# Order of the loads and sums at the head of an encoder kernel: x first, modulation pair by pair, half of the bias marks on ScalarE

## The chip, the cores and the metric

The kernel runs on one core of one Trainium2 chip. The metric is the time of one execution on the device in microseconds (us). Before the change it was 2237.97 us, the median of three runs (2234.70, 2237.97, 2239.76). The execution whose profile is shown here took 2236.12 us, and its span from the first to the last instruction was 2234.3 us.

## The reference, cut to what matters

The reference is a two-layer encoder trunk on 256 tokens of width 2048 in float32. Each sub-layer is modulated by a vector c. Only the parts that the change touches are given:

```python
cond = silu(c)
for l in range(2):
    mod = cond @ w_ada[l] + b_ada[l]              # 2048 -> 6 * 2048
    sh_a, sc_a, g_a, sh_m, sc_m, g_m = split(mod, 6)
    h = rmsnorm(x) * (1 + sc_a) + sh_a
    proj = h @ w_in[l]                            # 2048 -> 3904
    ...
    rel = positions[None, :] - positions[:, None]
    bias = rel_bias_table[t5_bucket(rel)]         # 32 buckets, 4 heads, same in both layers
    p = softmax(q @ k.T * scale + bias)
```

The bucket of a distance is found from its sign and its size. Distances 0 to 7 have a bucket each; the larger ones share buckets by ranges up to 128.

## The kernel before, in words

The 2048 features stand as 16 slices of 128 on the partitions, the 256 tokens on the free axis. The kernel is a stream of weights from HBM: SyncE (SP) issues nearly every DMA, in program order, into a ring of five tiles of 1 MB named `raw` (line 113 and 289). ScalarE (ACT) makes the upper part `hi` of each weight tile, VectorE (DVE) the rest `lo`, and TensorE (PE) multiplies the operand with both (lines 146, 147 and 182 to 184). A scheduler orders the instructions of each engine by its own forecast and puts in the semaphores; each engine then runs its list in order.

**Modulation.** `w_ada` is 192 tiles of 128 x 2048, and each is read once. DVE multiplies a tile with `cond` and sums along the row (`ada`, line 297), which gives 128 entries of one modulation vector; two such sums and a small addition (`mod`, lines 311 and 313) serve two slices. `ada_need` loads the tiles that the next step lacks, `ada(n)` loads n tiles in any case.

**Head.** `setup` loads c (`c_row`), spreads silu(c) over all partitions with four matmuls and four activations (`cond`, line 343), loads the small tables, then four `ada` tiles (`self.ada(4)`), then x in four parts, takes the squares of x on ACT (line 477) and their sums on DVE (line 478), and then ten more `ada` tiles (`LEAD`). The 14 tiles serve the shift and scale of slices 0 to 6.

**First input projection.** `norm_then_by_k` makes 1/rms (`rstd`, PE, ACT and DVE) and goes over eight pairs of slices, p = 0 to 7. Each pair needs four `ada` sums (two of the shift, two of the scale), then `modulated`: `ht` on DVE, `h` on ACT and DVE, and for p < 6 (`WHOLE`) `hf` on ACT. For these six pairs the weights are not split: four tiles `w` of 128 x 768 (line 228) go into PE as float32 (line 239), into buffers of the `hi` and `lo` tags. From p = 6 on they go through `hi` and `lo`.

**Fills.** After each pair one piece of setup is written: `lb` (lambdas, the start of the bias), then the four parts 0 to 3 of the bias, then the rope tables `r`. A part (`bias_part`) clamps the distances `rel` on DVE, and for eight groups of four buckets takes a square around the middle of the bucket (`sq`, ACT, line 428), compares it with the half width on DVE (a mark `oh` of 0 or 1, line 430) and multiplies the marks with the table on PE (lines 432 and 433). Four activations (line 435) then copy the result from PSUM to `bias`.

**Afterwards.** With p = 5 and 6, pieces of a later projection (`w_d`) are inserted; then come the remaining projections of layer 0 (`w_t`), interleaved with the attention scores (`psc`, line 943), which read k copied by ACT (line 272). From about 260 us on the kernel is a stream of weights whose order the change leaves as it is.

Of the kernel before, what the change touches and what calls it, by code (L numbers as in the profile page):

```python
# [13 lines left out]
AF = mybir.ActivationFunctionType  # L14
ALU = mybir.AluOpType
# [5 lines left out]
D = 2048  # L21
# [22 lines left out]
C_CB = 160  # L44
C_W2 = 168
# [26 lines left out]
def consts():  # L72
    c = np.zeros((P, NCONST), np.float32)
    p = np.arange(P)
    c[p, C_DELTA + p % 32] = 1.0
    c[p, C_PERM + (p ^ 32)] = 1.0
    for g in range(8):
        for r in range(4):
            b = 4 * g + r
            n = b % 16  # L80
            lo, hi = BUCKET_FROM[n], BUCKET_FROM[n + 1] - 1
            sign = -1.0 if b < 16 else 1.0
            rows = slice(32 * r, 32 * r + 32)
            if b == 16:
                c[rows, C_CB + g], c[rows, C_W2 + g] = 0.0, -1.0
            else:
                c[rows, C_CB + g] = -sign * (lo + hi) / 2.0
                c[rows, C_W2 + g] = ((hi - lo) / 2.0 + 0.25) ** 2
    c[:, C_FREQ] = np.asarray(INV_FREQ, np.float32)[p % 32]
    c[:, C_SGN] = np.where(p % 64 < 32, -1.0, 1.0)  # L90
    return c


EARLY = {5: (0,), 6: (1, 2)}
LEAD = 10
WHOLE = 6
NAHEAD = 6
NNORM = 12
# [6 lines left out]
class Trunk:  # L105
    def __init__(self, ctx, tc, io):
        self.nc, self.tc, self.io = tc.nc, tc, io
        pool = lambda name, bufs, **k: ctx.enter_context(tc.tile_pool(name=name, bufs=bufs, **k))
        self.fp = pool("fp", 1)
        self.wp = pool("wp", 4)  # L110
        self.up = pool("up", 40)
        self.tp = pool("tp", 6)
        self.cp = pool("cp", 1)
        self.sp = pool("sp", 8)
        self.ap = pool("ap", 6)
        self.pp = pool("pp", 8, space=bass.MemoryType.PSUM)
        self.ada_todo, self.ada_here, self.rate, self.credit = [], [], 0.0, 0.0
        self.n = 0

    def name(self, s):  # L120
        self.n += 1
        return f"{s}_{self.n}"
# [169 lines left out]
    def ada_sums(self, after=None):  # L292

        nc = self.nc
        for w, l, g, i in self.ada_here:
            acc = self.macc[l, g]
            ins = nc.vector.scalar_tensor_tensor(  # L297
                w, w, 1.0, self.cond, ALU.mult, ALU.mult, accum_out=acc[:, i : i + 1]
            )
            if after is not None:  # L300
                self.tc.add_manual_dep(
                    ins.ins, after.ins.name,
                    mybir.DependencyInfo(mybir.DependencyClass.NoSync, mybir.DependencyReason.DATA),
                    reason="issue order",
                )
            if i % 2:
                c = slice(i - 1, i + 1)
                v = V_BADA + 96 * l + NK * g + i
                b = self.vec[:, v - 1 : v + 1]
                if g % 3 == 1:  # L310
                    nc.vector.scalar_tensor_tensor(self.mod[l, g][:, c], acc[:, c], 1.0, b, ALU.add, ALU.add)
                else:
                    nc.vector.tensor_tensor(self.mod[l, g][:, c], acc[:, c], b, ALU.add)
        self.ada_here = []
# [14 lines left out]
    def setup(self):  # L329
        nc, io, cp = self.nc, self.io, self.cp  # L330
        self.ada_plan()
        self.cond = cp.tile([P, D], F32, name="cond")
        row = self.wp.tile([1, D], F32, tag="raw", name="c_row", bufs=5)
        nc.sync.dma_start(row, io["c"])
        self.mean = {}
        for n in (D, 2 * P):
            self.mean[n] = cp.tile([P, P], F32, name=f"mean{n}")
            nc.gpsimd.memset(self.mean[n], 1.0 / n)
        for j in range(4):
            c = slice(512 * j, 512 * j + 512)  # L340
            ps = self.bank("pc").rearrange("p a b -> p (a b)")
            nc.tensor.matmul(ps, self.mean[D][:1], row[:, c], start=True, stop=True)
            nc.scalar.activation(self.cond[:, c], ps, AF.Silu, scale=float(D))  # L343
        self.vec = cp.tile([P, NVEC], F32, name="vec")
        nc.sync.dma_start(self.vec, io["vec"])
        self.eps = cp.tile([P, 1], F32, name="eps")
        nc.gpsimd.memset(self.eps, EPS)
        self.K = cp.tile([P, NCONST], F32, name="K")
        nc.sync.dma_start(self.K, io["consts"])
        self.pos = cp.tile([P, T + 8], I32, name="pos")  # L350
        nc.sync.dma_start(self.pos, io["pos"])
        self.ident = cp.tile([P, P], F32, name="ident")
        make_identity(nc, self.ident)
        self.x = cp.tile([P, NK, T], F32, name="x")
        self.ada(4)
        for q in range(4):
            nc.sync.dma_start(self.x[:, 4 * q : 4 * q + 4], io["xT"][:, 4 * q : 4 * q + 4])
        acc = None
        for k in range(0, NK, 2):
            acc = self.sumsq(acc, self.x[:, k : k + 2])  # L360
        self.ada(LEAD)
        return acc

    def fills(self):
        m = {"l": self.lambdas, "r": self.rope_setup, "b": self.bias_setup}
# [45 lines left out]
    def bias_part(self, a):  # L411
        nc, K = self.nc, self.K
        fh, fl, lh, ll = self.bt
        half = lambda s, dt=F32: self.up.tile([P, 2 * T], dt, tag="u", name=self.name(s))
        r = self.u("rel")
        for t in range(2):
            j = 2 * a + t
            d = self.tp.tile([P, T], F32, tag="t", name=self.name("rt"))
            nc.vector.tensor_scalar(d, fh[:, :T], fh[:, T + j : T + j + 1], 65536.0, ALU.subtract, ALU.mult)
            nc.vector.scalar_tensor_tensor(  # L420
                r[:, t], fl[:, :T], fl[:, T + j : T + j + 1], d, ALU.subtract, ALU.add
            )
        nc.vector.tensor_scalar(r, r, -128.0, 128.0, ALU.max, ALU.min)
        ps = self.bank("pb")
        out = ps.rearrange("p a b -> p (a b)")
        for g in range(8):
            sq = self.t("sq")
            nc.scalar.activation(sq, r, AF.Square, bias=K[:, C_CB + g : C_CB + g + 1])
            oh = half("oh", F32R)
            nc.vector.tensor_scalar(oh, sq.rearrange("p a b -> p (a b)"), K[:, C_W2 + g : C_W2 + g + 1], None, ALU.is_le)  # L430
            c = slice((g % 4) * P, (g % 4) * P + P)
            nc.tensor.matmul(out, lh[g // 4][:, c], oh, start=g == 0, stop=False)
            nc.tensor.matmul(out, ll[g // 4][:, c], oh, start=False, stop=g == 7)
        for h in range(HD):
            nc.scalar.activation(self.bias[32 * a : 32 * a + 32, h], ps[32 * h : 32 * h + 32], AF.Copy, scale=-1.0)

    def rope_setup(self):
        nc, K, pos = self.nc, self.K, self.pos
# [115 lines left out]
    def modulated(self, r, k, sh, sc, whole=None):  # L554

        nc = self.nc
        t = self.t("ht")
        out = [self.parts("h") for _ in range(2)]
        for i, (hi, lo, _) in enumerate(out):
            c = slice(k + i, k + i + 1)  # L560
            nc.vector.scalar_tensor_tensor(t[:, i], self.x[:, k + i], sc[:, c], r, ALU.mult, ALU.mult)
            nc.scalar.activation(hi, t[:, i], AF.Identity, bias=sh[:, c])  # L562
            nc.vector.scalar_tensor_tensor(lo, t[:, i], sh[:, c], hi.bitcast(F32), ALU.add, ALU.subtract)  # L563
        if whole is not None:
            f = self.u("hf")
            for i in range(2):
                nc.scalar.activation(f[:, i], t[:, i], AF.Identity, bias=sh[:, k + i : k + i + 1])
                whole.append(f[:, i])
        return out

    def latent(self, vals, g):
# [15 lines left out]
    def norm_then_by_k(self, l, acc, sh, sc, src, n, nwhole, fill=(), early=()):  # L587


        r = self.rstd(acc, D)  # L590
        banks = self.open_banks(2 * n)
        h = []
        for p in range(8):
            k = 2 * p
            for g in (sh, sc):
                self.ada_need(l, g, k + 1)
            whole = [] if p < nwhole else None
            h += self.modulated(r, k, self.mod[l, sh], self.mod[l, sc], whole)
            self.by_k(banks, [src[l, p, b] for b in range(2)], h, k, NK, 2 * n, whole)
            if fill:  # L600
                fill.pop(0)()
            if p in early:
                early[p](h)
        return h, banks
# [532 lines left out]
```

## Time and profile before

| | |
|---|---|
| median of three runs | 2237.97 us (2234.70 to 2239.76) |
| profiled execution, its span | 2236.12 us, 2234.3 us |
| PE busy, share of the span | 2157.3 us, 97% |
| DVE busy | 1618.6 us, 72% |
| ACT busy | 1151.2 us, 52% |
| DMA | 585.40 MB, mean 262 GB/s |
| mean granted TensorE clock | 0.994 |

The times are those of one execution, taken by the hardware profiler. A row of the timeline gives the start and the length in us, the engine, the line of the kernel, the operation, the output and the inputs, the number of merged instructions, and in brackets how long the engine sat idle before it and what ended that. A row with several instructions gives the time from the first start to the last end. Consecutive instructions of one engine overlap a little, so the step from start to start is shorter than a length. A row by stretches gives the stretch, its length, the busy time of PE, PE's weight loads, DVE, ACT and GpSimd (with instructions), the granted clock, the busy share of the DMA engines and GB/s.

### The profile page before, as it was taken

What the parts mean: (1) busy time and instruction counts of PE and PEld (TensorE: products, weight loads), DVE (VectorE), ACT (ScalarE), POOL (GpSimd) and SP (SyncE); (2) the same over time, 40 slices, a digit from 0 to 9 for tenths busy, and PEclk for the clock granted to TensorE, in tenths of its full rate; (3) what the DMA queues carried; (4) which work ended last, traced back from release to release, by engine and by line L of the source; (5) the groups of instructions that cost most, each with busy time, mean ns of one, the idle gap of its engine ahead of it and who ended that gap; (6) DMA issues with size and microseconds to landing.
All of it is one profiled execution on the core that took longest, in us unless ns stands there. A gap on an engine that the chain in (4) does not pass through costs nothing.

```text
span 2234.3 us, 30873 instructions
## 1 busy us (share of the span) xinstructions
PE 2157.3 (97%) x12254; PEld 1899.1 (85%) x12254; DVE 1618.6 (72%) x2141; ACT 1151.2 (52%) x1705; POOL 25.3 (1%) x43
## 2 busy tenths in 40 slices
PE   2999999899999999999999999999999999999997
PEld 1899889898888888888888898999888888888886
DVE  7889778988778778777899876788545545544555
ACT  2655655346455355446455555647545535534643
POOL 0000000000000000000001000001000000000000
PEclk9999999999999999999999999999999999999999
DMA  9988677878888878888877765675554555555551
GB/s 370 342 328 302 246 282 301 334 282 334 331 306 322 315 303 322 330 309 320 320 269 282 262 257 215 239 288 201 198 198 175 202 190 191 191 200 189 188 189 57
DMA packets 84677, 585.40 MB, mean 262 GB/s; under 512 B 9394, under 2 KB 9778, under 8 KB 18482
## 3 DMA queue, kind: packets, MB, share of 16 engines
q1 hardware_dynamic: 84530, 583.42, 70.4%
q8 instruction: 96, 1.57, 0.3%
q14 instruction: 51, 0.41, 0.0%
HBM read 581.28 MB, written 2.10 MB: 261 GB/s over the span
## 4 chain that ended last, share of the span: by engine, by line
PE 91%; DVE 5%; DMA 1%; issue 1%; ACT 1%; SPq 0%; DVEq 0%; ACTq 0%
PE ps L203 21%; PE ps L206 11%; PE py L843 10%; PE py L841 10%; PE py L845 10%; PE pk L183 2%; PE ps L183 2%; PE ps L182 2%; PE ps L184 2%; PE pk L184 2%; PE pk L182 2%; PE pk L239 2%; DVE ada L297 2%; PE pv L253 1%; PE pv L254 1%; PE pv L255 1%
## 5 line engine op out<-in xcount | busy, mean ns | idle before, releaser
L147 DVE TENSOR_TENSOR lo<-raw,hi 128x1024 fp32r<-128x1024 f32 (+1 forms) x720 | 851.3, 1195 | 486.4 <-ACT hi L146 331.0
L146 ACT ACTIVATE hi<-raw 128x1024 fp32r<-128x1024 f32 (+1 forms) x720 | 742.6, 1036 | 690.7 <-PE py L845 370.2
L203 PE MATMUL ps<-h,hi 128*128 128x512 f32 x2016 | 472.9, 391 | 0.0
L297 DVE SCALAR_TENSOR_TENSOR ada<-ada,cond 128x2048 f32<-128x2048 f32 x192 | 437.9, 2284 | 6.9 <-ACT cond L343 6.9
L203 PEld LDWEIGHTS ps<-h,hi 128*128 128x128 f32 x2016 | 375.0, 188 | 75.8 <-DVE h L563 0.2
L841 PE MATMUL py<-hi,hid 128*128 128x512 f32 x1024 | 326.0, 389 | 0.0
L843 PE MATMUL py<-lo,hid 128*128 128x512 f32 x1024 | 326.0, 389 | 0.0
L845 PE MATMUL py<-hi,hid 128*128 128x512 f32 x1024 | 325.7, 389 | 0.0
L206 PEld LDWEIGHTS ps<-h,lo 128*128 128x128 f32 x2016 | 250.5, 192 | 5.0
L206 PE MATMUL ps<-h,lo 128*128 128x256 f32 x2016 | 252.0, 283 | 0.0
L843 PEld LDWEIGHTS py<-lo,hid 128*128 128x128 f32 x1024 | 192.2, 188 | 40.5 <-DVE lo L147 0.7
L845 PEld LDWEIGHTS py<-hi,hid 128*128 128x128 f32 x1024 | 192.2, 188 | 40.0
L841 PEld LDWEIGHTS py<-hi,hid 128*128 128x128 f32 x1024 | 191.7, 188 | 39.1
L879 ACT ACTIVATE sum<-ps 128x256 f32<-128x256 f32 x110 | 42.1, 383 | 116.4 <-PE ps L206 115.9
L182 PE MATMUL pk<-h,hi 128*128 128x256 f32 x304 | 86.6, 288 | 6.3 <-ACT h L562 6.3
L183 PE MATMUL pk<-h,hi 128*128 128x256 f32 x304 | 87.0, 287 | 0.9 <-DVE h L563 0.7
L184 PE MATMUL pk<-h,lo 128*128 128x256 f32 x304 | 86.8, 286 | 0.0
L239 PE MATMUL pk<-hf,w 128*128 128x256 f32 x288 | 65.2, 388 | 21.2 <-DMA w<-in_w_a 21.2
L176 DVE TENSOR_TENSOR hid<-relu,hid 128x256 fp32r<-128x256 f32 x128 | 48.3, 420 | 47.4 <-ACT hid L175 47.4
L239 PEld LDWEIGHTS pk<-hf,w 128*128 128x128 f32 x288 | 55.9, 195 | 29.9 <-issue 21.9
L182 PEld LDWEIGHTS pk<-h,hi 128*128 128x128 f32 x304 | 58.9, 195 | 6.9 <-ACT h L562 6.9
L183 PEld LDWEIGHTS pk<-h,hi 128*128 128x128 f32 x304 | 59.4, 195 | 1.3 <-DVE h L563 1.3
(226 smaller groups left out, 2792.6 us busy)
## 6 DMA issues: line engine op xcount, KB each, us to landing
raw<-in_w_m SPq DMA_DIRECT2D x238, 1024.0 KB, 4.8
ada<-in_w_ada SPq DMA_DIRECT2D x192, 1024.0 KB, 4.9
raw<-in_w_ob SPq DMA_DIRECT2D x24, 1024.0 KB, 4.9
raw<-in_w_dv SPq DMA_DIRECT2D x16, 1024.0 KB, 4.8
raw<-in_w_q SPq DMA_DIRECT2D x16, 1024.0 KB, 4.8
raw<-in_w_n SPq DMA_DIRECT2D x16, 768.0 KB, 6.0
w<-in_w_a SPq DMA_DIRECT2D x24, 384.0 KB, 6.0
raw<-in_w_a SPq DMA_DIRECT2D x12, 768.0 KB, 5.2
```

The lines of the kernel that those rows point to most:

```text
L146: nc.scalar.activation(hi, v, AF.Copy)
L147: ins = nc.vector.tensor_tensor(lo, v, hi.bitcast(F32), ALU.subtract)
L182: mm(ps, hi, x[0], start=first, stop=False, skip_group_check=shared)
L183: mm(ps, hi, x[1], start=False, stop=False, skip_group_check=shared)
L184: mm(ps, lo, x[0], start=False, stop=last, skip_group_check=shared)
L203: mm(ps.rearrange("p a b -> p (a b)"), part(w, 0, k), both, start=k == 0, stop=False)
L206: mm(ps[:, 0], part(w, 1, k), x, start=False, stop=k == nk - 1)
L239: self.nc.tensor.matmul(ps, w[i][:, j * P : j * P + P], whole[i], start=first, stop=last, skip_group_check=True)
L297: ins = nc.vector.scalar_tensor_tensor(w, w, 1.0, self.cond, ALU.mult, ALU.mult, accum_out=acc[:, i : i + 1])
L841: mm(o, xh[:, tok], hi[:, part[j]], start=start, stop=False)
L843: mm(o, xh[:, tok], lo[:, part[j]], start=False, stop=False)
L845: mm(o, xl[:, tok], hi[:, part[j]], start=False, stop=stop)
```

## The change

- x is loaded right after the small tables, ahead of every `ada` tile, and 1/rms is made in `setup`. `ada(4)` and `ada(LEAD)` are gone: each pair's four `ada` tiles are loaded by `ada_need` just ahead of that pair's weights.
- In each group of marks g with g % 4 < 2 (groups 0, 1, 4 and 5, whose buckets hold one distance each) the mark is relu(1 - sq), made by ACT, instead of the comparison on DVE. The constants `C_W2` are changed to suit.
- The four copies from PSUM to `bias` are no longer issued behind the part's matmuls, but by `bias_out`, in order behind the next pair's `hf` on ACT.
- `follow` holds the ordering that `ada_sums` already used.

The lines of the changed kernel stand some rows off: 428 for the squares becomes 422, the marks on ACT are 426 and on DVE 428, the copies to `bias` 441, `ht` 577, `h` 578 and 579, `hf` 583, `mod` 307 and 309.

```diff
             if b == 16:
-                c[rows, C_CB + g], c[rows, C_W2 + g] = 0.0, -1.0
+                c[rows, C_CB + g], c[rows, C_W2 + g] = 0.0, 0.0
             else:
                 c[rows, C_CB + g] = -sign * (lo + hi) / 2.0
-                c[rows, C_W2 + g] = ((hi - lo) / 2.0 + 0.25) ** 2
+                c[rows, C_W2 + g] = 1.0 if n < 8 else ((hi - lo) / 2.0 + 0.25) ** 2
...
         self.x = cp.tile([P, NK, T], F32, name="x")
-        self.ada(4)
         for q in range(4):
             nc.sync.dma_start(self.x[:, 4 * q : 4 * q + 4], io["xT"][:, 4 * q : 4 * q + 4])
         acc = None
         for k in range(0, NK, 2):
             acc = self.sumsq(acc, self.x[:, k : k + 2])
-        self.ada(LEAD)
-        return acc
+        return self.rstd(acc, D)
...
             oh = half("oh", F32R)
-            nc.vector.tensor_scalar(oh, sq.rearrange("p a b -> p (a b)"), K[:, C_W2 + g : C_W2 + g + 1], None, ALU.is_le)
+            flat, edge = sq.rearrange("p a b -> p (a b)"), K[:, C_W2 + g : C_W2 + g + 1]
+            if g % 4 < 2:
+                nc.scalar.activation(oh, flat, AF.Relu, bias=edge, scale=-1.0)
+            else:
+                nc.vector.tensor_scalar(oh, flat, edge, None, ALU.is_le)
...
-        for h in range(HD):
-            nc.scalar.activation(self.bias[32 * a : 32 * a + 32, h], ps[32 * h : 32 * h + 32], AF.Copy, scale=-1.0)
+        self.evict = a, ps
+
+    def bias_out(self, after):
+
+        if self.evict is None:
+            return
+        a, ps = self.evict
+        self.evict = None
+        for h in range(HD):
+            ins = self.nc.scalar.activation(
+                self.bias[32 * a : 32 * a + 32, h], ps[32 * h : 32 * h + 32], AF.Copy, scale=-1.0
+            )
+            self.follow(ins, after)
...
             for i in range(2):
-                nc.scalar.activation(f[:, i], t[:, i], AF.Identity, bias=sh[:, k + i : k + i + 1])
+                ins = nc.scalar.activation(f[:, i], t[:, i], AF.Identity, bias=sh[:, k + i : k + i + 1])
                 whole.append(f[:, i])
+            self.bias_out(ins)
...
-        r = self.rstd(acc, D)
+        r = self.rstd(acc, D) if l or sh else acc
```

The rows below are from the orders of the two programs, with the buffer numbers of the tiles. The first two are on ACT, from the pair p = 4 (`h`, `hf`) to the marks of bias part 3 behind it. Before:

```order
L562 ACTIVATE h_637<-ht_636,mod_79 128x256
L562 ACTIVATE h_638<-ht_636,mod_79 128x256
L567 ACTIVATE hf_645<-ht_636,mod_79 128x256 x2
L435 ACTIVATE bias<-pb_457 32x512 x4
L428 ACTIVATE sq_689<-rel_680,K 128x512
L428 ACTIVATE sq_695<-rel_680,K 128x512
L428 ACTIVATE sq_701<-rel_680,K 128x512
L428 ACTIVATE sq_707<-rel_680,K 128x512
L428 ACTIVATE sq_713<-rel_680,K 128x512
L428 ACTIVATE sq_719<-rel_680,K 128x512
L428 ACTIVATE sq_725<-rel_680,K 128x512
L428 ACTIVATE sq_731<-rel_680,K 128x512
```

Now, from the copies to `bias` on:

```order
L441 ACTIVATE bias<-pb_569 32x512 x4
L422 ACTIVATE sq_689<-rel_680,K 128x512
L422 ACTIVATE sq_695<-rel_680,K 128x512
L426 ACTIVATE oh_691<-sq_689,K 128x512
L426 ACTIVATE oh_697<-sq_695,K 128x512
L422 ACTIVATE sq_701<-rel_680,K 128x512
L422 ACTIVATE sq_707<-rel_680,K 128x512
L422 ACTIVATE sq_713<-rel_680,K 128x512
L422 ACTIVATE sq_719<-rel_680,K 128x512
L426 ACTIVATE oh_715<-sq_713,K 128x512
L426 ACTIVATE oh_721<-sq_719,K 128x512
L422 ACTIVATE sq_725<-rel_680,K 128x512
```

Behind the last row comes one more square, `sq_731`. Four marks stand among the squares, and the copies ahead of them are those of the part just before (`pb_569`), not of the one before that (`pb_457`).

On DVE, the marks of bias part 2, behind pair p = 3, and the way to `ht` of pair p = 4. Before:

```order
L430 TENSOR_SCALAR oh_584<-sq_582,K 128x512
L430 TENSOR_SCALAR oh_590<-sq_588,K 128x512
L430 TENSOR_SCALAR oh_596<-sq_594,K 128x512
L297 SCALAR_TENSOR_TENSOR ada_625,macc_80<-ada_625,cond 128x2048
L430 TENSOR_SCALAR oh_602<-sq_600,K 128x512
L430 TENSOR_SCALAR oh_608<-sq_606,K 128x512
L430 TENSOR_SCALAR oh_614<-sq_612,K 128x512
L313 TENSOR_TENSOR mod_79<-macc_80,vec 128x2
L297 SCALAR_TENSOR_TENSOR ada_629,macc_82<-ada_629,cond 128x2048
L297 SCALAR_TENSOR_TENSOR ada_632,macc_82<-ada_632,cond 128x2048
L311 SCALAR_TENSOR_TENSOR mod_81<-macc_82,vec 128x2
L561 SCALAR_TENSOR_TENSOR ht_636<-x,mod_81,rstd_215 128x256 x2
```

Now:

```order
L297 SCALAR_TENSOR_TENSOR ada_618,macc_80<-ada_618,cond 128x2048
L428 TENSOR_SCALAR oh_584<-sq_582,K 128x512
L428 TENSOR_SCALAR oh_590<-sq_588,K 128x512
L297 SCALAR_TENSOR_TENSOR ada_621,macc_80<-ada_621,cond 128x2048
L428 TENSOR_SCALAR oh_608<-sq_606,K 128x512
L309 TENSOR_TENSOR mod_79<-macc_80,vec 128x2
L428 TENSOR_SCALAR oh_614<-sq_612,K 128x512
L297 SCALAR_TENSOR_TENSOR ada_625,macc_82<-ada_625,cond 128x2048
L297 SCALAR_TENSOR_TENSOR ada_628,macc_82<-ada_628,cond 128x2048
L307 SCALAR_TENSOR_TENSOR mod_81<-macc_82,vec 128x2
L577 SCALAR_TENSOR_TENSOR ht_632<-x,mod_81,rstd_166 128x256 x2
```

Four marks remain; the last two, of ACT's last two squares, stand ahead of the last two `ada` sums and of the next `ht`.

On DVE, the rests of the weights `w_d` (`lo` of 128 x 1024) inserted behind pair p = 6, and the way to `ht` of p = 7 (`ht_1128`). Before:

```order
L147 TENSOR_TENSOR lo_1001<-raw_998,hi_1000 128x1024
L297 SCALAR_TENSOR_TENSOR ada_1114,macc_80<-ada_1114,cond 128x2048
L147 TENSOR_TENSOR lo_1005<-raw_998,hi_1004 128x1024
L147 TENSOR_TENSOR lo_1059<-raw_1056,hi_1058 128x1024
L297 SCALAR_TENSOR_TENSOR ada_1117,macc_80<-ada_1117,cond 128x2048
L147 TENSOR_TENSOR lo_1063<-raw_1056,hi_1062 128x1024
```

Now:

```order
L147 TENSOR_TENSOR lo_1001<-raw_998,hi_1000 128x1024
L147 TENSOR_TENSOR lo_1005<-raw_998,hi_1004 128x1024
L147 TENSOR_TENSOR lo_1059<-raw_1056,hi_1058 128x1024
L297 SCALAR_TENSOR_TENSOR ada_1114,macc_80<-ada_1114,cond 128x2048
L147 TENSOR_TENSOR lo_1063<-raw_1056,hi_1062 128x1024
L297 SCALAR_TENSOR_TENSOR ada_1117,macc_80<-ada_1117,cond 128x2048
```

Both `ada` sums moved behind one or two more `lo`. Two more sums and `ht_1128` follow in both programs; before, two `lo` of 128 x 768 stood among them, and now these come behind `ht_1128`. From here to about 260 us the scheduler has moved a number of `ada` sums, scores and softmax steps by a few places. On SP only the rows of the first six pairs are moved.

More of the change, by code (lines that the diff above doesn't have):

```diff
@@ L94 @@
 EARLY = {5: (0,), 6: (1, 2)}
-LEAD = 10
 WHOLE = 6
@@ L300, in ada_sums @@
             if after is not None:
[L301 to L305, printed above, removed]
+                self.follow(ins, after)
             if i % 2:
@@ L433, in bias_part, with follow @@
             nc.tensor.matmul(out, ll[g // 4][:, c], oh, start=False, stop=g == 7)
-        for h in range(HD):
-            nc.scalar.activation(self.bias[32 * a : 32 * a + 32, h], ps[32 * h : 32 * h + 32], AF.Copy, scale=-1.0)
+        self.evict = a, ps
[3 more added lines that the diff above has]
+        a, ps = self.evict
+        self.evict = None
+        for h in range(HD):
+            ins = self.nc.scalar.activation(
+                self.bias[32 * a : 32 * a + 32, h], ps[32 * h : 32 * h + 32], AF.Copy, scale=-1.0
+            )
+            self.follow(ins, after)
+    def follow(self, ins, after):
+        self.tc.add_manual_dep(
+            ins.ins, after.ins.name,
+            mybir.DependencyInfo(mybir.DependencyClass.NoSync, mybir.DependencyReason.DATA),
+            reason="issue order",
+        )
     def rope_setup(self):
```

## The prediction

> **What bounds the kernel now.** I read the stretches first (columns: stretch, length, then PE, weight loads, DVE, ACT and GpSimd busy, granted clock, DMA share, GB/s).
>
> ```profile
> 48.00:130.00 82.00, 81.56 (x376) 70.99 (x377) 74.72 (x133) 44.84 (x77) 0.53 (x1) 1.00 0.84 313
> 130.00:200.00 70.00, 68.47 (x551) 67.15 (x550) 63.59 (x85) 39.04 (x55) 0.00 (x0) 1.00 0.86 329
> 200.00:260.00 60.00, 51.40 (x345) 46.85 (x345) 51.78 (x101) 30.86 (x61) 0.00 (x0) 0.97 0.77 292
> 260.00:300.00 40.00, 40.00 (x210) 33.98 (x209) 27.76 (x47) 23.62 (x49) 0.00 (x0) 1.00 0.68 254
> ```
>
> From 260 us on PE is full, and the change leaves its order alone there: what counts is how much earlier the work stands at 260. Next come PE's waits from 40 to 420 us (what waited, for whom: us in total, times, longest).
>
> ```profile
> PE pk L239 <- DMA w<-in_w_a: 21.2, 1, 21.2
> PE psc L943 <- ACT k L272: 5.9, 3, 2.2
> PE pk L183 <- DVE h L563: 0.7, 1, 0.7
> ```
>
> The 21.2 us before the first projection look like the prize. But the third row says that at pair 6 PE waits for DVE anyway:
>
> ```profile
> 113.48 0.88 DVE L561 SCALAR_TENSOR_TENSOR ht<-x,mod,rstd 128x256 f32<-128x256 f32 x2
> 132.74 0.88 DVE L561 SCALAR_TENSOR_TENSOR ht<-x,mod,rstd 128x256 f32<-128x256 f32 x2
> 133.82 0.38 PE L182 MATMUL pk<-h,hi 128*128 128x256 f32 x1 [0.45 <-ACT h L562]
> 134.94 0.39 PE L183 MATMUL pk<-h,hi 128*128 128x256 f32 x1 [0.73 <-DVE h L563]
> ```
>
> So an earlier PE start is worth only as much as `ht` of pair 5 (113.48) and of pair 6 (132.74) come earlier. Between the two DVE is nearly full and its order is unchanged. The sum is therefore made on DVE's and ACT's time to `ht` of pair 5.
>
> **The change part by part.** *Start.* The timeline of before gives the prices:
>
> ```profile
> 9.87 0.60 ACT L343 ACTIVATE cond<-pc 128x512 f32<-128x512 f32 x1 [1.11 <-PE pc L342]
> 16.25 0.63 ACT L474 ACTIVATE acc<-x 128x512 f32<-128x512 f32 x1 [5.79 <-DMA x<-in_xT]
> 16.79 4.41 ACT L477 ACTIVATE sqx<-x 128x512 f32<-128x512 f32 x7
> 19.62 5.46 DVE L478 TENSOR_TENSOR acc<-acc,sqx 128x512 f32<-128x512 f32 x7
> 25.13 2.08 PE L487 MATMUL pn<-acc,mean 128*128 128x256 f32 x4 [15.30 <-DVE acc L478]
> 29.09 1.75 DVE L490 RECIPROCAL rstd<-rstd 128x256 f32<-128x256 f32 x1 [1.81 <-ACT rstd L489]
> 10.00:20.00 10.00, 0.00 (x0) 0.00 (x0) 9.47 (x11) 3.91 (x7) 0.00 (x0) 1.00 1.02 419
> ```
>
> x arrives at 16.25 behind 4.2 MB; at 419 GB/s those took 10.0 us, so x's quarters now land at about 6.2, 7.5, 8.7 and 10.0, and four `ada` tiles by 20. The last `cond` ends at 10.47 and six squares stand behind it: 6 x 0.63 to 14.2. DVE's sums (0.78 each) end at 15.8. Two `ada` sums (2.21 each, from the loop's rows below) to 20.2; `rstd` is ready for DVE 25.13 to 29.09 = 3.96 after the matmul's start, 19.9, so no wait; reciprocal 1.68; two more `ada`, of which the last to `ht` takes 2.53 (below): 20.2 + 1.7 + 2.2 + 2.5 gives `ht` of pair 0 at 26.7. DMA is no limit here: the first `w` lands behind 4 MB of `ada`, by about 21.
>
> *Pair 0 to pair 1.* The start of the bias, the lambdas and four sums lie between (the last two rows are from the chain of waits):
>
> ```profile
> 41.28 0.29 DVE L394 TENSOR_SCALAR ih<-pos 128x264 int32<-128x264 int32 x1
> 42.11 0.68 DVE L403 TENSOR_TENSOR lsc<-vec,K 128x512 f32<-128x512 f32 x1
> 42.83 0.63 ACT L406 ACTIVATE lsch<-lsc 128x512 fp32r<-128x512 f32 x1 [5.41 <-DVE lsc L403]
> 48.44 12.57 PE L239 MATMUL pk<-hf,w 128*128 128x256 f32 x48 [21.23 <-DMA w<-in_w_a]
> ...
> 61.12 10.47 PE pk L239 x48
> 75.26 10.36 PE pk L239 x48
> ```
>
> On DVE: `ht` and `h` 1.6, four conversions 0.8, two `lsc` and one rest 0.6 each, 0.7 of waiting for `lsch`, so 31.9 with the small steps; one more rest, then three sums and 2.53: `ht` of pair 1 at 42.0. Beside it, PE starts at `hf`, 1.8 behind `ht` (28.5), and takes 12.57: `pl` at 41.1 and `lam` at about 41.7, just in time. The old place of the `ada` loads cost PE the time to 48.44, but what was paid there is not free now: the sums of pair 1 follow in line.
>
> *The loop of pairs 1 to 5.* One pair of before:
>
> ```profile
> 95.43 0.88 DVE L561 SCALAR_TENSOR_TENSOR ht<-x,mod,rstd 128x256 f32<-128x256 f32 x2
> 98.59 0.43 DVE L423 TENSOR_SCALAR rel<-rel 128x512 f32<-128x512 f32 x1
> 100.86 1.10 DVE L430 TENSOR_SCALAR oh<-sq,K 128x512 fp32r<-128x512 f32 x2 [1.84 <-ACT sq L428]
> 101.87 2.28 DVE L297 SCALAR_TENSOR_TENSOR ada<-ada,cond 128x2048 f32<-128x2048 f32 x1
> 104.08 2.46 DVE L430 TENSOR_SCALAR oh<-sq,K 128x512 fp32r<-128x512 f32 x6
> 110.95 2.28 DVE L297 SCALAR_TENSOR_TENSOR ada<-ada,cond 128x2048 f32<-128x2048 f32 x1
> ...
> 96.77 0.89 ACT L567 ACTIVATE hf<-ht,mod 128x256 f32<-128x256 f32 x2
> 97.68 2.39 ACT L435 ACTIVATE bias<-pb 32x512 f32<-32x512 f32 x4
> 100.10 5.01 ACT L428 ACTIVATE sq<-rel,K 128x512 f32<-128x512 f32 x8
> L428 ACT ACTIVATE sq<-rel,K x32: 704/708/724, 59.5 to 104.4; 128x512 f32<-128x512 f32 x32
> ```
>
> This one took 113.48 - 95.43 = 18.05. Now from `ht` = 0: ACT does `hf`, then the copies, and begins its squares at 100.10 - 95.43 = 4.67 (the step now stands behind `hf` in every pair, as here). The step is (5.01 - 0.71) / 7 = 0.614, and twelve operations stand there instead of eight. The new relu has no row of its own; it reads SBUF with a bias per partition as the square does, so I take 0.614. Below it lies 0.54 (16.25 to 16.79, no such bias); above, 0.71, if it did not overlap. The marks left on DVE need the 5th, 6th, 11th and 12th operation. The 6th is done at 4.67 + 5 x 0.614 + 0.71 = 8.45, mark to 8.9, `ada` to 11.1; the 12th at 12.13, mark to 12.6, `ada` to 14.8, and from the last `ada` to `ht` 113.48 - 110.95 = 2.53: **17.33**. DVE's own work is 3.6 + 3 x 2.21 + 4 x 0.41 + 2.53 = 14.4; nearly 3 us are waiting for ACT. Taking 1.64 us of marks off DVE puts 2.46 us ahead of the marks that stay. The Trainium skill (ScalarE: Activation LUTs, "Rules for kernel authors") speaks against this edit: it tells one to do a relu on VectorE, not on ScalarE. By that rule all eight marks would stay on DVE, 14.4 + 1.6 = 16.0 a pair with the squares done at 9.7, and pair 5 would come up to 5 us earlier still; the rows' 0.41 against 0.614 agree with it for one mark, and my sum goes by the rows. Pair 1 has no copies ahead, and its squares begin 1.0 earlier, held by `rel`: 16.33. So `ht` of pair 5 is at 42.0 + 16.33 + 3 x 17.33 = 110.3, **3.1 earlier** than 113.48. PE's 10.4 a pair and the 75.26 - 71.59 = 3.7 of bias matmuls behind it leave it idle 3 us each time, and the copies' source is ready 3 us before they come up. DMA's 5.8 MB a pair take 13.8 us at 419 GB/s, less than 17.3.
>
> *Pairs 6 and 7.* With the same DVE order PE resumes at 131.8. Behind it, two `ada` sums moved behind `lo` that wait for `hi`, paced by PE:
>
> ```profile
> 139.31 1.06 ACT L146 ACTIVATE hi<-raw 128x1024 fp32r<-128x1024 f32 x1 [1.10 <-PE pk L183]
> 143.63 1.06 ACT L146 ACTIVATE hi<-raw 128x1024 fp32r<-128x1024 f32 x1 [1.10 <-PE pk L183]
> 153.64 0.88 DVE L561 SCALAR_TENSOR_TENSOR ht<-x,mod,rstd 128x256 f32<-128x256 f32 x2
> ```
>
> In the clock of before: third `lo` 142.6 to 143.7, `ada` to 145.9, `lo` to 147.1, two `ada` to 151.5 and 2.53: 154.0 instead of 153.64, 0.4 lost. Then PE is full to about 200, and the shift stands: **-2.7 us**. The removed `LEAD` loads and the ordering helper cost nothing of their own: the DMA traffic is the same.
>
> The sum against the profiled execution: 2236.1 - 2.7 = 2233.4. The median lies 1.85 above that execution, so I predict 2237.97 - 2.7 = 2235.3. A measurement of this kernel tells about 0.2%, 4.5 us, from no change; the likeliest case is below that.
>
> **The rivals.** *A cold clock at pair 6.* PE now idles 2 to 3 us before each pair. Speed was lost after such a gap once before:
>
> ```profile
> 205.08 1.18 PE L943 MATMUL psc<-k,q 128*128 128x256 f32 x4 [2.22 <-ACT k L272]
> 206.00:208.00 2.00, 2.00 (x11) 1.97 (x11) 2.00 (x6) 0.60 (x2) 0.00 (x0) 0.51 0.92 336
> 136.00:138.00 2.00, 2.00 (x19) 2.00 (x18) 1.88 (x3) 1.22 (x2) 0.00 (x0) 1.00 1.01 426
> ```
>
> Eight of 19 matmuls are missing in two microseconds at clock 0.51, 0.84 us, and about as much again in the next two: 1.7 us. In pairs 1 to 5 the idle time absorbs that; at pair 6 it would go to the end: -1.0, 2237.0. The Trainium skill (TensorE: Matmul & The Clock Gate, "What's actually happening") says that the clock halves after an idle window of about 3.4 us; by that page my gap of 2.3 us before pair 6 would mostly be too short, though the trace's 2.22 us sufficed. I keep it a rival.
>
> *The waits of the scores vanish* (faster). The 5.9 us of PE waiting for `k` sit in a stage whose order has been shuffled. If ACT gets to `k` in time: -2.7 - 5.9 = -8.6, 2229.4. For it speaks that DVE has four fewer marks a part; against it, that those marks are done long before 200 us.
>
> *DVE's own work sets the loop* (much faster): if ACT's twelve operations did not hold it, 14.4 a pair, `ht` of pair 5 at 99.6, and with PE's 14.1 a pair about -13: 2225. ACT's list in order speaks against it.
>
> *Slower.* From 170 us on, `ada` sums stand later on DVE, each holding one of five `raw` tiles, and SP issues in order. If each of the three waits for `k` grew by one sum, 2.21, the price is 6.6: +3.9, 2241.9, and 2243.6 with a cold clock. It decides once more than 2.7 us are added. Against it: DVE's total there is unchanged, and the `lo` that come earlier free tiles too.
>
> *The change does nothing*: the start is moved, and the loop and the stage before 260 give all of it back: 2238.
>
> **How the numbers follow.** Forecast (-2.7, own range -5 to -1) 0.42; cold clock 0.14; nothing 0.10; waits vanish 0.16; DVE's loop 0.05; slower 0.13. Of the forecast some 0.10 lie beyond 4.5 us: faster 0.10 + 0.16 + 0.05 = 0.31, slower by over 0.2% 0.13, the rest 0.56. The relu's bounds (16 of them, 0.54 to 0.71) give -1.2 to +1.5, the start 1 us either way. The range, 2230.5 to 2241, takes these in, most of the vanishing waits and part of the slower case.
>
> **What would show it.** First `w` matmul near 28.5; `ht` of pairs 1 and 5 near 42 and 110; about 17.3 us from pair to pair with DVE waiting for ACT's squares; PE waiting some 2 us at pair 6. A step near 14.5 would make the prediction wrong, as would waits at `psc` far from 5.9 us.

## The result and the profile after

The changed kernel takes 2228.13 us (median of five, 2227.89 to 2228.23) against 2237.97 us of the kernel before in the same session: a ratio of 0.9956, with a 95% interval of 0.9942 to 0.9971. In a later session it was 2228.19 us against 2236.80, 0.9957 (0.9945 to 0.997). So the change saves 9 to 10 us, not the 2.7 that were forecast. The profiled execution took 2228.13 us, its span is 2226.4 us; by spans the two profiles differ by 7.9 us, and it is these 7.9 that the rows are to explain (the profiled execution of before lay 1.85 us below its median). Nearly all of it is there by 320 us, where both programs have long had the same order again. The same instruction of ACT, before (first row) and now, 7.78 us earlier:

```profile
318.58 0.60 ACT L170 ACTIVATE moh<-pom 128x512 fp32r<-128x512 f32 x1 [0.65 <-PE pom L1026]
310.80 0.60 ACT L170 ACTIVATE moh<-pom 128x512 fp32r<-128x512 f32 x1 [0.65 <-PE pom L1043]
```

First the head. These are the first multiplications of DVE (`ht`) of pairs 0, 1, 4, 5 and 7 in the changed kernel:

```profile
26.39 0.88 DVE L577 SCALAR_TENSOR_TENSOR ht<-x,mod,rstd 128x256 f32<-128x256 f32 x2
41.64 0.88 DVE L577 SCALAR_TENSOR_TENSOR ht<-x,mod,rstd 128x256 f32<-128x256 f32 x2
...
92.34 0.88 DVE L577 SCALAR_TENSOR_TENSOR ht<-x,mod,rstd 128x256 f32<-128x256 f32 x2
109.63 0.88 DVE L577 SCALAR_TENSOR_TENSOR ht<-x,mod,rstd 128x256 f32<-128x256 f32 x2
...
150.02 0.88 DVE L577 SCALAR_TENSOR_TENSOR ht<-x,mod,rstd 128x256 f32<-128x256 f32 x2
```

Pair 5 stands at 109.63 against 113.48, 3.85 us earlier, and pair 7 at 150.02 against 153.64, 3.6 earlier. What held the loop is seen between pairs 3 and 4, on ACT (first fence) and DVE (second):

```profile
77.30 2.39 ACT L441 ACTIVATE bias<-pb 32x512 f32<-32x512 f32 x4
79.71 1.33 ACT L422 ACTIVATE sq<-rel,K 128x512 f32<-128x512 f32 x2
80.95 1.32 ACT L426 ACTIVATE oh<-sq,K 128x512 fp32r<-128x512 f32 x2
82.18 2.54 ACT L422 ACTIVATE sq<-rel,K 128x512 f32<-128x512 f32 x4
84.63 1.32 ACT L426 ACTIVATE oh<-sq,K 128x512 fp32r<-128x512 f32 x2
85.85 1.32 ACT L422 ACTIVATE sq<-rel,K 128x512 f32<-128x512 f32 x2
```

```profile
82.92 1.10 DVE L428 TENSOR_SCALAR oh<-sq,K 128x512 fp32r<-128x512 f32 x2 [2.07 <-ACT sq L422]
```

ACT goes through its twelve squares and relus without a pause, 0.61 to 0.62 us from start to start (from 79.71 to 85.85 are ten steps), and DVE's bracket names ACT's squares. PE idles before every pair. Its matmuls of pairs 0 and 2 to 5:

```profile
28.27 12.60 PE L239 MATMUL pk<-hf,w 128*128 128x256 f32 x48 [10.50 <-ACT hf L583]
59.90 10.63 PE L239 MATMUL pk<-hf,w 128*128 128x256 f32 x48 [2.08 <-ACT hf L583]
76.93 12.17 PE L239 MATMUL pk<-hf,w 128*128 128x256 f32 x48 [2.74 <-ACT hf L583]
94.22 10.63 PE L239 MATMUL pk<-hf,w 128*128 128x256 f32 x48 [1.44 <-ACT hf L583]
111.51 13.64 PE L239 MATMUL pk<-hf,w 128*128 128x256 f32 x48 [3.01 <-ACT hf L583]
```

So far it is the forecast. The rest lies behind the head. One stretch (columns as in the prediction), and PE's waits from 40 to 420 us:

```profile
200.00:260.00 60.00, 56.81 (x406) 52.72 (x405) 54.50 (x102) 36.83 (x73) 0.00 (x0) 1.00 0.83 314
```

```profile
PE pk L239 <- ACT hf L583: 11.8, 5, 3.0
PE psc L960 <- DVE mx L961: 2.5, 2, 1.5
PE psm L1026 <- DVE sm L1028: 1.7, 1, 1.7
PE ps L184 <- DVE lo L147: 1.0, 1, 1.0
PE pk L183 <- DVE h L579: 0.5, 1, 0.5
```

From 200 to 260 us PE is busy for 56.81 us where it was busy for 51.40, and `psc` no longer waits for `k` at all: the 5.9 us are gone. The same few instructions of ACT in both traces tell why. Before:

```profile
198.23 1.05 ACT L146 ACTIVATE hi<-raw 128x1024 fp32r<-128x1024 f32 x1
203.49 1.06 ACT L146 ACTIVATE hi<-raw 128x1024 fp32r<-128x1024 f32 x1 [4.21 <-DMA raw<-in_w_t]
204.45 0.58 ACT L272 ACTIVATE k<-ps 128x512 f32<-128x512 f32 x1
```

After:

```profile
197.01 1.06 ACT L146 ACTIVATE hi<-raw 128x1024 fp32r<-128x1024 f32 x1 [0.30 <-PE ps L183]
197.98 0.58 ACT L272 ACTIVATE k<-ps 128x512 f32<-128x512 f32 x1
...
202.98 1.04 ACT L146 ACTIVATE hi<-raw 128x1024 fp32r<-128x1024 f32 x1
```

Before, the first of the three copies of `k` stands behind the conversion of one more weight tile, and that conversion sits 4.21 us waiting for its DMA. After, the copy goes first. It isn't only a shift in time; ACT's order has changed. From the orders of the two programs, before and after:

```
130 L146 ACTIVATE hi_1826<-raw_1824 128x1024
131 L272 ACTIVATE k_1571<-ps_1391 128x512

145 L272 ACTIVATE k_1571<-ps_1391 128x512
146 L947 ACTIVATE s_1637,tot_1643<-s_1637,mx_1638 128x256
147 L146 ACTIVATE hi_1826<-raw_1824 128x1024
```

The other two copies (`k_1728` before the conversion of `raw_1992`, `k_1885` before that of `raw_2068`) moved in the same way. The conversions that they stood behind did not wait for a DMA: the second waited 1.83 us for PE, the third not at all.

The 7.9 us can be added up. At pair 7 the head is 3.6 ahead. From 155 to 420 us PE waited 8.8 us before (5.9, 2.3, 0.4 and 0.2) and lost 1.7 to the clock; now it waits 5.2 (2.5, 1.7 and 1.0) and loses 1.7 to the clock, which stands at 0.50 from 190 to 192 us. That is 3.6 more, 7.2 together; the other 0.7 was not traced.

### The profile page after: what moved, and what is told of

Same layout as the page of the kernel before. It is cut to its first block, busy times and chain, and to the rows that moved or that the text cites. A ratio compares the mean times of both kernels' runs of the same rounds, so it can differ in the third digit from the quotient of the medians.

```text
span 2226.4 us, 30855 instructions
## 1 busy us (share of the span) xinstructions
PE 2162.7 (97%) x12254; PEld 1902.9 (85%) x12254; DVE 1612.4 (72%) x2125; ACT 1159.9 (52%) x1721; POOL 25.3 (1%) x43
## 4 chain that ended last, share of the span: by engine, by line
PE 90%; DVE 7%; ACT 2%; issue 1%; DMA 0%; DVEq 0%; ACTq 0%
PE ps L203 21%; PE ps L206 11%; PE py L860 10%; PE py L858 10%; PE py L862 10%; DVE ada L297 3%; PE ps L184 2%; PE ps L182 2%; PE ps L183 2%; PE pk L183 2%; PE pk L182 2%; PE pk L184 2%; PE pv L255 1%; PE pv L253 1%; PE pv L254 1%; DVE lo L147 1%
## 5 line engine op out<-in xcount | busy, mean ns | idle before, releaser
L239 PE MATMUL pk<-hf,w 128*128 128x256 f32 x288 | 70.3, 409 | 22.3 <-ACT hf L583 22.3
```

The source lines that it names most:

```text
L239: self.nc.tensor.matmul(ps, w[i][:, j * P : j * P + P], whole[i], start=first, stop=last, skip_group_check=True)
```

## The experiments

**Is it the order on ACT, or the earlier start?** Two theories. T1: the order alone made PE wait. T2: everything stands some 4 us earlier, and the waits went with that. One run puts the new order into the kernel before, one the old order into the changed kernel; each has the other's head.

```diff
 # e3: the kernel before; e4: the changed kernel, with the two instructions of follow exchanged
+    def weighed(self, hi):                  # called for the first hi of each weight tile
+        for k in self.ks:                   # [copy of k, tiles until its turn: 4, 4, 3]
+            k[1] -= 1
+            if k[1] == 0:
+                self.follow(hi, k[0])       # e4: self.follow(k[0], hi)
```

Expected of the kernel before with the new order:

> The kernel before, its head untouched, with three orders forced on ACT between 200 and 235 us: each of the three k copies of the scores goes ahead of the conversion of the next weight tile, as it stands in the changed kernel. Theory T1 (the order on ACT alone made PE wait for k): PE's waits at psc for k fall from 5.9 us to under 1, ht of pair 7 stays at 153.6, and the total is about 4 us less than before, near 2234. T2 (the waits went because all work stood earlier): the waits stay near 5.9 us or move to another releaser, total as before, 2238.

Measured: 2229.71 us against 2237.22, 0.9969 (0.9958 to 0.9981). The head is where it was, with `ht` of pair 7 at 154.05 (before: 153.64). ACT's rows and PE's waits from 155 to 420 us of this run:

```profile
198.79 1.05 ACT L147 ACTIVATE hi<-raw 128x1024 fp32r<-128x1024 f32 x1
199.74 0.57 ACT L275 ACTIVATE k<-ps 128x512 f32<-128x512 f32 x1
203.61 2.01 ACT L147 ACTIVATE hi<-raw 128x1024 fp32r<-128x1024 f32 x2 [3.30 <-DMA raw<-in_w_t]
```

```profile
PE psc L960 <- DVE mx L961: 2.1, 4, 1.1
PE psm L1026 <- DVE sm L1028: 1.7, 1, 1.7
PE pk L186 <- DVE h L579: 0.4, 1, 0.4
```

The tile still comes late (3.30 us of waiting), but `k` is no longer queued behind it. T1 said 4 us; the run gave 7.5. The waits for `k` were too small a sum, because two more things went with the old order. One is another wait, of before:

```profile
PE pqr L916 <- ACT qr L272: 2.3, 1, 2.3
```

The other is the low clock behind the gap of 2.22 us, 1.7 us by the prediction's own rows. By spans: 5.9 + 2.3 + 0.4 + 0.2 of waits and 1.7 of clock before, 2.1 + 1.7 + 0.4 now, a difference of 6.3, and the spans are 2234.3 and 2228.0. The part of the clock differs between executions: from 200 to 260 us its mean is 0.97 in the profile of before and 1.00 here, but 0.94 and 0.91 in the profiles of two runs below that have the old order.

This run parts the stage from the head, but not the three copies from the rest of the stage. With the three orders forced, the scheduler also moved conversions, softmax steps, `ada` sums and the two copies `qr` between about 200 and 263 us, much as in the changed kernel.

Expected of the changed kernel with the old order:

> The changed kernel with the old order forced on ACT at the three k copies: each behind the conversion of the next weight tile. Theory T1: PE waits again some 2 us before each of the three scores, total about +4 us against the changed kernel, near 2232, with ht of pair 7 unchanged at 150.0. T2: waits stay as in the changed kernel, total 2228.

Measured: 2235.67 us against 2237.22, 0.9994 (0.9985 to 1.0002). Nearly all of the gain is gone, with pair 5 at 109.70 us as in the changed kernel.

```profile
202.48 1.06 ACT L147 ACTIVATE hi<-raw 128x1024 fp32r<-128x1024 f32 x1 [3.48 <-DMA raw<-in_w_t]
203.44 0.58 ACT L275 ACTIVATE k<-ps 128x512 f32<-128x512 f32 x1
```

```profile
PE psc L970 <- ACT k L275: 4.1, 2, 2.7
PE pqr L943 <- ACT qr L275: 2.3, 1, 2.3
```

Both ways round the order of this stage, as the three forced copies bring it about, is worth 7.5 us and the head 1.5 (e4 against before; 1.6 between e3 and the changed kernel). T2 is refuted: an earlier start with the old order waits again.

**Which part brings the order, and is there gain without it?** The old start with the new marks and evictions:

```diff
+        self.ada(4)
         for q in range(4):
             nc.sync.dma_start(self.x[:, 4 * q : 4 * q + 4], io["xT"][:, 4 * q : 4 * q + 4])
...
-        return self.rstd(acc, D)
+        self.ada(LEAD)
+        return acc
```

> The old start (four ada tiles ahead of x, ten more and the sum of squares behind it, rstd in its old place) with the relus and the evictions of the changed kernel. The order on ACT from 155 to 235 us comes out as in the kernel before, the three k copies behind the next conversion. Theory A: PE is full from 48 us on whatever ACT and DVE do beside it, so marks and evictions alone can win at most the 1.2 us that PE waited at pair 6; theory T1: the waits for k stay near 6 us; together 2236 to 2237.5, no difference from before. Rival B (the marks and evictions bring the gain by themselves): 2230 or less.

Measured: 2237.70 us against 2236.80, 0.9998 (0.9989 to 1.0007). Pair 5 stands at 112.21, pair 7 at 153.64 as before the change, and the waits for `k` are back:

```profile
PE psc L963 <- ACT k L273: 5.7, 3, 2.1
```

Marks and evictions alone bring nothing. It is the start (x first, sums pair by pair) that turns the scheduler's order at 200 us: the runs below, all with the new start, have the new order, and the two programs with the old start have the old one unless it is forced. Why the scheduler's forecast turns there was not examined.

**Do the relus pay?** All eight marks on DVE again:

```diff
-            if g % 4 < 2:
-                nc.scalar.activation(oh, flat, AF.Relu, bias=edge, scale=-1.0)
-            else:
-                nc.vector.tensor_scalar(oh, flat, edge, None, ALU.is_le)
+            nc.vector.tensor_scalar(oh, flat, edge, None, ALU.is_le)
```

> The changed kernel with all eight marks of a part on DVE again (is_le, the old constants); x first, the pair-by-pair sums and the place of the evictions stay. Theory A (ACT's relus pay, because on DVE the marks wait for squares that stand behind the four copies): a pair takes 3.6 us to rel, waits to 6.4 for the second square, and does six marks, three sums and the rest to about 18.0 us instead of 17.3; ht of pair 5 comes 2.4 us later than with the relus (109.6 to about 112), the total is +2 to +2.5 us against the changed kernel (about 2230.5). Rival B (relu belongs on VectorE): the marks of 0.41 us on DVE leave a pair of 16.0 us, ht of pair 5 comes 4 to 5 us earlier, near 105, and the total is about 2224. Theory T1 of the stage (order of ACT) and T2 (mere shift) both leave the waits of the scores small here.

Measured: 2230.91 us, 0.9974 (0.9964 to 0.9985) of before; 2.8 us above the changed kernel. One pair of it:

```profile
99.91 1.10 DVE L425 TENSOR_SCALAR oh<-sq,K 128x512 fp32r<-128x512 f32 x2 [1.83 <-ACT sq L422]
...
112.54 0.88 DVE L574 SCALAR_TENSOR_TENSOR ht<-x,mod,rstd 128x256 f32<-128x256 f32 x2
```

A pair takes 18.04 us (94.50 to 112.54), as Theory A had it. The four extra marks cost 1.6 us of DVE, and the wait of 1.83 us for ACT's first squares stays.

**What is the place of the evictions worth?** They are issued right behind the part's matmuls again:

```diff
-        self.evict = a, ps
+        for h in range(HD):
+            nc.scalar.activation(self.bias[32 * a : 32 * a + 32, h], ps[32 * h : 32 * h + 32], AF.Copy, scale=-1.0)
```

> The changed kernel with the four bias copies of a part left free to be placed, as before the change: ACT does them between the two halves of h, ahead of hf. Theory A: hf, and with it PE's start of each pair, comes 2.4 us later; in pairs 1 to 4 PE's idle time of 2 to 3 us takes that in, at pair 5 it goes to the end, less the 0.5 us that PE waits at pair 6; DVE waits 0.3 us a pair for the second h: +2 to +3 us against the changed kernel, about 2230.5 to 2231. Rival B: the place of the copies costs nothing, since ACT does the same twelve operations and four copies a pair: 2228.

Measured: 2238.97 us, 1.0004 (0.9995 to 1.0013) of before, 10.8 us above the changed kernel. Both theories missed: I had expected 2 to 3. ACT's rows of pair 4, PE's of the same pair, and the clock in the middle of them:

```profile
99.19 2.38 ACT L433 ACTIVATE bias<-pb 32x512 f32<-32x512 f32 x4 [3.17 <-PE pb L431]
...
102.56 13.38 PE L239 MATMUL pk<-hf,w 128*128 128x256 f32 x48 [3.41 <-ACT hf L584]
...
104.00:106.00 2.00, 2.00 (x6) 1.62 (x5) 1.69 (x2) 2.00 (x4) 0.00 (x0) 0.50 0.00 0
```

The copies stand ahead of `hf`, and wait themselves for PE's last bias matmul, which stands behind PE's 48 matmuls, which wait for the `hf` of the pair before. That is a ring: 13.0 + 4.0 + 3.4 = 20.4 us, and the next group starts at 123.01, 20.45 later. In each turn PE idles for 3.41 us, and behind that the matmuls begin at a clock of 0.50. The kernel before has no such ring: its copies behind p = 4 are of the part before the last (`pb_457`), and they wait for nothing (the row at 97.68 in the prediction). So this run is more than the old place again. To part ring and clock, the next run keeps the ring and fills the gap:

```diff
+        self.spare = self.bank("pb")        # the next part's bank
+        for i in range(12):                 # sums that nothing reads
+            nc.tensor.matmul(self.spare.rearrange("p a b -> p (a b)"), ll[1][:, c], oh, start=True, stop=True)
```

> The run with the evictions at their old place (2238.97 us), and behind the bias matmuls of each part twelve more of them into a spare bank, whose sums nothing reads; PE does them in the 3.41 us in which it waits for hf. In that run a pair is a ring: 48 matmuls (13.0 us at the low clock), bias matmuls (4.0), copies and hf (3.4), 20.45 together. Theory C (ring and clock): the ring stays, but without the gap the clock stays at 1.00, the 48 matmuls take 10.3 instead of 13.0 us, a pair 17.7; ht of pair 5 near 109.5 instead of 115.4, the total 5 to 7 us less, 2232 to 2234, and the scatter of 7 us between executions falls to 1 or 2. Rival D (the clock does not depend on the gap): the 48 matmuls stay at 13.4 us and the total near 2239. Rival E (no ring; something else, such as the weights' transfers, held these pairs): the matmuls are fast but ht of pair 5 stays near 115.

Measured: 2230.77 us, 0.9975 (0.9965 to 0.9984) of before, 8.2 us less than without the fillers. The fillers of two parts and the matmuls behind the second (`ht` of pair 5 is at 110.37):

```profile
76.24 2.88 PE L434 MATMUL pb<-oh,lscl 128*128 128x512 f32 x12
93.96 2.88 PE L434 MATMUL pb<-oh,lscl 128*128 128x512 f32 x12
97.54 10.63 PE L239 MATMUL pk<-hf,w 128*128 128x256 f32 x48 [0.69 <-ACT hf L587]
```

From 76.24 to 93.96 are 17.72 us, the ring at full clock, as Theory C had it. So of the 10.8 us 8.2 go with the idle gap and its low clock, and 2.6 stay with the ring. The scatter fell from 7.0 to 3.3 us, less than expected.

**Does ACT's list hold the loop, and can it be shortened?** The four groups whose marks DVE makes are squared first:

```diff
-        for g in range(8):
+        for n, g in enumerate((2, 3, 6, 7, 0, 1, 4, 5)):
```

> The changed kernel with the groups of a part in another order: ACT squares first the four whose marks DVE makes, then the four that it marks itself, so that DVE no longer waits behind relus (the bias sum is added in another order of groups). Theory A (ACT's list held the loop): DVE waits only for the second square, 6.0 us after ht, then two marks, a sum, two marks, two sums and 2.53 us: 16.4 us a pair instead of 17.3, pair 1 15.3; ht of pair 5 near 105.8 instead of 109.6, PE's gaps shrink to 2 us. Since the lead of the head shrank from 4.0 to 1.7 us on its way through the stage at 185 to 200 us, I expect 1.5 to 4 us less than the changed kernel in all, 2224 to 2226.6. Rival B (PE or DMA, not ACT, held the loop): ht of pair 5 stays within 1 us of 109.6 and the total is 2228.

Measured: 2225.26 us, 0.9945 (0.9932 to 0.9957) of before and 2.9 us below the changed kernel in the same session. With the copies behind the first four squares as well:

```diff
+            if n == 3:
+                self.bias_out(ins)          # ins: the fourth square
...
-            self.bias_out(ins)
+            if k == 2 * WHOLE - 2:
+                self.bias_out(ins)
```

> As the run with the groups reordered, and the four copies of the part before go behind the first four squares of the next part instead of behind hf. Theory A: the first marks come 0.7 us behind rel instead of 1.8, a pair takes 15.5 us (DVE's own work 14.4), ht of pair 5 near 103.5, and PE's gaps are 1.4 us, too short for the clock to fall; 3 to 6 us less than the changed kernel, 2222 to 2225. Rival B (the stage at 185 to 260 us, not the head, sets what arrives): the total stays within 1 us of 2228 though pair 5 comes earlier.

Measured: 2222.74 us, 0.9935 (0.9923 to 0.9948) of before, 5.4 us below the changed kernel: the best of all runs. The first fence is the first reordering, the second the one with the copies:

```profile
75.74 12.31 PE L239 MATMUL pk<-hf,w 128*128 128x256 f32 x48 [2.01 <-ACT hf L583]
...
90.45 0.88 DVE L577 SCALAR_TENSOR_TENSOR ht<-x,mod,rstd 128x256 f32<-128x256 f32 x2
...
107.03 0.88 DVE L577 SCALAR_TENSOR_TENSOR ht<-x,mod,rstd 128x256 f32<-128x256 f32 x2
```

```profile
88.83 0.88 DVE L579 SCALAR_TENSOR_TENSOR ht<-x,mod,rstd 128x256 f32<-128x256 f32 x2
...
93.20 1.71 DVE L430 TENSOR_SCALAR oh<-sq,K 128x512 fp32r<-128x512 f32 x3 [0.79 <-ACT sq L422]
...
104.57 0.88 DVE L579 SCALAR_TENSOR_TENSOR ht<-x,mod,rstd 128x256 f32<-128x256 f32 x2
106.45 10.63 PE L239 MATMUL pk<-hf,w 128*128 128x256 f32 x48 [1.44 <-ACT hf L585]
```

The pair falls from 17.29 to 16.58 and 15.74 us (expected 16.4 and 15.5), DVE's wait for its first squares from 1.83 to 0.79 us between the two runs, pair 5 from 109.6 to 107.0 and 104.6, and 5.1 us of lead there were worth 5.4 at the end.

The changed kernel once more, in the session of the last three:

> The changed kernel as it is, on the same chip as the three others of this call: 2228 us by every theory.

It took 2228.19 us. In this profiled execution pair 5 is at 109.81, but pair 7 at 151.61 instead of 150.02. Between them PE waits 1.9 us at pair 6 (first row), and behind that the clock is low (second row, a stretch):

```profile
PE pk L182 <- ACT h L578: 1.9, 1, 1.9
132.00:134.00 2.00, 2.00 (x11) 2.00 (x11) 2.00 (x3) 0.62 (x2) 0.00 (x0) 0.50 1.02 430
```

So the place of pair 7 differs by 1.6 us from one execution to the next, and this one is the usual: 22.7 us from `ht` of pair 6 to that of pair 7, against 22.6 to 22.7 in four other runs with the new start, 21.3 in the first profile and 20.9 before. At `moh` the two executions stand alike all the same (310.80 and 310.88), since the first one's clock fell later, at 190 us.

## Why the prediction was wrong

- *Start.* Right: `ht` of pair 0 at 26.39 (26.7), of pair 1 at 41.64 (42.0), PE's first matmul at 28.27 (28.5).
- *The loop.* Right: pair 1 took 16.38 us (16.33), the later ones 17.03 to 17.29 (17.33), and DVE waited for ACT's squares. The relu has the square's step, as assumed. `ht` of pair 5 came 3.85 us earlier (3.1; the prediction's own terms give 3.2).
- *Keeping the marks on DVE.* The rule of the Trainium skill (ScalarE: Activation LUTs, "Rules for kernel authors": a relu on VectorE rather than on ScalarE) was priced at 16.0 us a pair; measured are 18.04, so here the measurement decides against it. The price left out that DVE then stands waiting for ACT's first squares all the same (1.83 us).
- *Pairs 6 and 7.* The term was too small in most executions: 0.4 us of loss were forecast, 3.85 became 3.6 in the first profile, but 2.0 in the second, whose step from pair 6 to pair 7 four other runs with the new start share. In the first, PE waited only 0.5 us at pair 6: the gap of 3.01 us ahead of pair 5 lowered the clock, the 48 matmuls took longer, and that filled the wait. In the second it waited 1.9 us, as forecast (some 2), and the clock fell behind that, as the rival of the cold clock had it.
- *"Then PE is full to about 200, and the shift stands."* This is the step that failed. It took the stage from 196 to 262 us with its 5.9 us of waits over from before, though the order of ACT there had been dealt anew. The runs show in its place: the three copies of `k` now stand ahead of the conversion of the next weight tile, the first of which waits for its DMA, and with what the scheduler moved behind them this order is worth 7.5 us. The head by itself, at the old order, is worth 1.5 us where 2.7 were forecast, and the interval of that run includes no change at all.
- *The rival that came true* is "the waits of the scores vanish": -8.6 by its sum. That this sum comes near is in part luck: it left out the wait of `pqr`, 2.3 us, and the clock, 1.7, and counted 2.7 for a head worth 1.5. The reason given for it was not the right one either: it named DVE's marks, and it was ACT's order. The argument against it, that the marks are done long before 200 us, met only that reason. What would have told: the two orders of ACT at that place, set beside the row of 203.49, in which `hi` waits 4.21 us ahead of `k`.
- *Open:* 1.0 and 1.0 us that PE waits at 187 to 190 in the changed kernel (`psc` for `mx`, `ps` for `lo`; before 0.2) take back part of the head's lead. They are seen in the traces with the new start, the one with the old order forced too, and no run removed them. In the first profile the clock fell behind them (0.50 from 190 to 192 us), in the second it did not.

## What to carry to other kernels

When a scheduler orders the program, an edit at the head can deal out anew the order of a stage 150 us later; compare the orders of both programs wherever the trace of before shows a wait, above all where a short copy that PE waits for stands behind a conversion that waits for a DMA. An eviction that waits for PE must not stand ahead of the operand that PE waits for: the two close a ring, and every turn of it adds its idle gap. Of work shared out between two engines, the part that the other engine finishes should come first.

## What the runs showed of the clock

The 48 matmuls of a pair take 10.63 us at full clock. Behind gaps of 1.4 to 1.7 us they still did in every row looked at. Behind gaps of 2.0 to 3.0 us some did and some did not: 10.63 after 2.08 in the first profile of the changed kernel and 12.31 after 2.06 at the same place in the second; 10.63 after 2.96 with the marks on DVE, 12.31 after 2.01 in the run with the reordered groups. After 3.41 they took 13.38. So the length of a gap alone does not decide. One fall of the clock lasted some 3.4 us in the second profile (0.2 us of it before 132, 2.0 to 134 and 1.2 behind that, by the mean clock of 0.95, 0.50 and 0.69 in these stretches), which at half the clock is 1.7 us of work. The Trainium skill (TensorE: Matmul & The Clock Gate, "What's actually happening") has the clock halve after an idle window of about 3.4 us that runs freely. Half the clock agrees with these rows, and a window that runs freely would fit that equal gaps cost differently, though no run shows the window itself; a gap of 3.4 us is not needed, since 2.01 us was enough to lose 1.7.
